# A decoder layer on one Trainium2 core: more of the up-projection's first half done ahead, and the modulation weights asked for by running estimates

## The chip, the cores and the metric

The kernel runs on one core of a Trainium2 chip. The metric is the device time of one execution in microseconds (us). The kernel before takes 1207.88 us (median of 3 runs, 1207.71 to 1208.54).

The engines have short names: PE is the matrix engine, PEld its loading of stationary operands, DVE the vector engine, ACT the scalar engine, SP the engine that issues the transfers. Each engine runs its own instructions strictly in the order in which they stand in its stream, and waits on semaphores for the others.

## The reference, cut to what matters

One layer for 256 tokens of width 2048. A conditioning vector gives six rows of modulation (shift, scale, gate, twice). There are two kinds of attention heads, one output projection, and a gated feed-forward part of width 5504 with a causal convolution of width 3.

```python
mod = silu(c) @ w_ada + b_ada                       # 2048 -> 12288 = 96 columns of 128
sh1, sc1, g1, sh2, sc2, g2 = split(mod, 6)
h = rmsnorm(x) * (1 + sc1) + sh1
q_sb, k_sb, v_sb, q_ds, k_ds, v_ds, q_ix, k_ix, w_ix = split(h @ w_in)
o_sb = stick_breaking_attention(q_sb, k_sb, v_sb)   # 8 heads
o_ds = dsa_attention(...)                           # 8 heads, keys chosen by an indexer, top 64
x  = x + g1 * (concat(rmsnorm(o_sb), rmsnorm(o_ds)) @ w_out)
h2 = rmsnorm(x) * (1 + sc2) + sh2
u  = h2 @ w_up                                      # 2 x 5504 columns: 43 pairs of 128 (gate, value)
uc = causal_conv3(u); a = silu(uc_gate) * uc_value
x  = x + g2 * (a @ w_down)
out = rmsnorm(x)
```

## The kernel before

**Matmuls.** Every large product is taken in fp32r as three matmuls: high by high part, high by low, low by high. A weight load is 1 MB, a tile of 128 x 2048. `split` cuts it in halves of 128 x 1024: ACT casts the high part (L145), DVE subtracts for the low part (L146), each into one of three buffers.

**Transfers.** All weight loads stand in one queue of SP in program order, with four buffers (`load`, L135 to L138). A load is issued when the buffer's former user is done.

**Modulation.** It is 96 columns, in groups of four. A column in DVE's form (`ada`, L216) is one 1 MB load `wa` and one DVE instruction over 128 x 2048 (L218). A group in PE's form (`ada_pe`, L187, for the groups listed in `PEG`) is four 1 MB loads `wg`, each with matmuls of 512 columns into `ap` (L195), then a copy on ACT, four transposes into `aq` (L203) and a small DVE sum. Both forms bring 4 MB per group. Which ones come when is set by `pump`: at its step i it emits as many columns and quarters as the strings of `PLAN` say, and after their end as `RATE` says. `need(j)` emits whatever is still missing.

**Order of the stages.** Projection pass 0 over half of the contraction (wA0 to wA7), with B, V and QK of that half. Then pass 1 (wA8 to wA15), B1, and the indexer with its top-k on DVE (`rel`, L548, L571, L572). V10 and V11 follow, then the sparse attention (`kdsp`, `qdsp`, `lg`), and QK8 to QK15 with the eight stick-breaking heads (`sb_head`, L659). The output projection O begins with the first halves of output tiles m = 0 to 3 from `odh`, `odl`. In the program `rms_b` named `rsb` and `norm_o` come next; they make `osh`, `osl` for the second halves. Then come the residual, `r2`, and the modulated `h2`.

**Up-projection U.** Each pair f has two loads, `wU f 0` for k 0 to 7 and `wU f 1` for k 8 to 15. For the first G0 = 8 pairs the first halves are done ahead, each pair in its own PSUM bank, while the later columns of `h2` are still being made. The second halves then add to the same banks. These pairs use `trn`: three matmuls of 256 columns for each k and half. The other pairs use `fold`: one of 512 columns and one of 256, with two banks, and ACT and DVE add the two parts of a bank (L837, L838). After that come the convolution (L844, L848), SiLU, product, and split into `aT`. W, the down-projection, and the final norm end the kernel.

The scheduler arranges each engine's instructions itself from the program and its dependencies, so a step's place in a stream is not its place in the program.

Of the kernel before, what the change touches and what calls it, by code (L numbers as in the profile page):

```python
# [19 lines left out]
P = 128  # L20
# [22 lines left out]

PEG = [4, 40, 48, 76, 52]

PARTS = [8, 8]

PLAN = ("40300000010011011020201102100000000000000010222000110020002020001010003012011002101000000000100000213",
        "00000000000000000000000000000110010000001200000100001200003100000000000000110100001010001000001000000")

RATE = (0.4, 0.7)


@with_exitstack
def layer(ctx: ExitStack, tc: tile.TileContext, a, out):
# [78 lines left out]

    def load(src, n, name):  # L135
        w = wp.tile([P, 2048], F32, name=name, tag="raw", bufs=4)
        DMA.dma_start(out=w[:, 0:n], in_=src)
        return w  # L138
# [10 lines left out]
    def nat(pt, xh, xl, wh, wl, first, last):  # L149

        T.matmul(pt, lhsT=xh, rhs=wh, start=first, stop=False)  # L151
        T.matmul(pt, lhsT=xh, rhs=wl, start=False, stop=False)
        T.matmul(pt, lhsT=xl, rhs=wh, start=False, stop=last)

    def fold(steps):

        for pt, x, wh, _, first, _ in steps:
            T.matmul(pt, lhsT=wh, rhs=x, start=first, stop=False)  # L160
        for pt, x, _, wl, _, last in steps:
            T.matmul(pt[:, 1, :], lhsT=wl, rhs=x[:, 0, :], start=False, stop=last)  # L162

    def trn(pt, xh, xl, wh, wl, first, last):

        T.matmul(pt, lhsT=wh, rhs=xh, start=first, stop=False)  # L166
        T.matmul(pt, lhsT=wh, rhs=xl, start=False, stop=False)  # L167
        T.matmul(pt, lhsT=wl, rhs=xh, start=False, stop=last)  # L168
# [18 lines left out]
    def ada_pe(j0, q, st={}):  # L187
# [3 lines left out]
        pt = st[j0]  # L191
        w = load(a["wg"][PEG.index(j0), q], 2048, f"wg{j0}{q}")
        for j in range(4):
# [22 lines left out]
    def ada(j):  # L216
        w = load(a["wa"][j], 2048, f"wa{j}")
        i = V.scalar_tensor_tensor(out=w, in0=w, scalar=1.0, in1=scb, op0=ALU.mult, op1=ALU.mult,  # L218
                                   accum_out=mod[:, j:j + 1])
        if after[0] is not None:  # L220
            order(i, after[0])
# [79 lines left out]
    def modulate(dh, dl, x, am, rb, sh, name, variant):  # L301

        h = s2([P, S], F32, name)
        if not variant:
            V.scalar_tensor_tensor(out=h, in0=x, scalar=am, in1=rb, op0=ALU.mult, op1=ALU.mult)
            A.activation(dh, h, AF.Identity, bias=sh)
            V.scalar_tensor_tensor(out=dl, in0=h, scalar=sh, in1=dh.bitcast(F32), op0=ALU.add, op1=ALU.subtract)
            return
# [30 lines left out]
    def put(half, dst, src, scale=1.0):  # L339
        if half == 0:  # L340
            if scale == 1.0:
                A.copy(out=dst, in_=src)
            else:
                A.mul(out=dst, in_=src, mul=scale)
        elif scale == 1.0:
            V.tensor_tensor(out=dst, in0=src, in1=dst, op=ALU.add)
# [3 lines left out]
    pending, pend_pe = [], []  # L350
    credit = [0.0, 0.0]
    emitted = set()
# [15 lines left out]

    step = [0]

    def pump():
        i = step[0]
        step[0] += 1
        for c, l in enumerate((pending, pend_pe)):
            if i < len(PLAN[c]):
                n = int(PLAN[c][i])
            else:
                credit[c] += RATE[c]
                n = int(credit[c])
                credit[c] -= n  # L380
            for _ in range(min(n, len(l))):
                emit(l)

# [155 lines left out]
    for t in range(NT):  # L539
# [4 lines left out]
        for g in range(8 // npb):  # L544
# [6 lines left out]
            for par_ in range(2):  # L551
                rl = s2([P, npb, L], F32, f"rl{t}{g}{par_}")
                A.activation(rl, pts[par_].rearrange("p (n l) -> p n l", n=npb), AF.Relu)  # L553
                for j in range(npb):
# [9 lines left out]
                    else:  # L564
                        V.scalar_tensor_tensor(out=sacc[par_], in0=rl[:, j, :], scalar=wix[:, t, h:h + 1],  # L565
                                               in1=sacc[par_], op0=ALU.mult, op1=ALU.add)
        V.tensor_tensor(out=sacc[0], in0=sacc[0], in1=sacc[1], op=ALU.add)
        cur, nxt = sacc
        for r in range(8):
# [26 lines left out]
    for t in range(NT):  # L596
# [29 lines left out]
        for g in range(2):  # L626
# [6 lines left out]
            for j in range(4):  # L633
                h = 4 * g + j
                A.activation(od[:, h, t * P:(t + 1) * P], pv[:, j, :], AF.Copy, scale=par[:, PDG + h:PDG + h + 1])
        pump()
    for w_ in (4, 2):
# [6 lines left out]
    def norm_o(o, rb_, oh, ol):  # L644
        for h in range(0, NH, 4):
# [3 lines left out]
            A.copy(out=oh[:, sl, :], in_=o[:, sl, :])  # L649
            V.tensor_tensor(out=ol[:, sl, :], in0=o[:, sl, :], in1=oh[:, sl, :].bitcast(F32), op=ALU.subtract)  # L650

    norm_o(od, rdb, odh, odl)
# [5 lines left out]

    def sb_head(h):  # L659
        q = qk[h // 4][:, (h % 4) * 2, :]  # L660
        k = qk[h // 4][:, (h % 4) * 2 + 1, :]
# [65 lines left out]
    def resid(dst, acc, gate, res, sqsum, k, name):  # L727

        resid_i[0] = V.scalar_tensor_tensor(out=dst, in0=acc, scalar=gate, in1=res, op0=ALU.mult, op1=ALU.add)  # L729
        if k == 0:  # L730
# [56 lines left out]
    aT = []  # L787

    G0 = 8
    uacc = {}  # L790

    def do_U(f, i):

        if i == 0:
            uacc[f] = [bank(f"U{f}{gv}") for gv in range(2)] if f >= G0 else bank(f"U{f}")
        w = load(a["wU"][f, i], 2048, f"wU{f}{i}")
        for gv in range(2):
# [6 lines left out]
            for j in range(8):  # L804
# [5 lines left out]
                else:  # L810
                    trn(uacc[f][:, gv, :], x[:, 0, :], x[:, 1, :], wh[:, sl], wl[:, sl], k == 0 and gv == 0,
                        k == KT - 1 and gv == 1)
            fold(steps)
# [7 lines left out]
    for f in range(G0):  # L821
        do_U(f, 0)
        pump()
        if f >= 3:
# [3 lines left out]
    for f in range(FT):  # L828
# [3 lines left out]
        acc = uacc.pop(f)  # L832
        pump()
        if f >= G0:
# [4 lines left out]
        else:  # L839
            u = acc  # L840
        uc = s2([P, 2, S], F32, f"uc{f}")
# [119 lines left out]
```

## Time and profile before

| what | value |
|---|---|
| median of 3 runs | 1207.88 us |
| profiled execution, its own time | 1209.0 us |
| its span from first to last instruction | 1207.2 us |
| mean granted PE clock | 0.982 |
| PE busy | 1154.3 us, 7120 matmuls |
| DVE busy | 886.8 us |
| ACT busy | 630.6 us |
| loads `wa` / `wg` | 76 / 20 of 1 MB each |
| bytes read | 300.24 MB |

A busy time is a sum over the whole span; matmuls are pipelined, so a stretch in which PE is busy throughout can still hold fewer matmuls than it could. The chain of waits names, from the last instruction backward, what each step waited for. In the timeline a row's brackets give the idle time of the engine before the instruction, and the instruction that ended it.

### The profile page before, as it was taken

The numbers are of one execution on the slowest core, as the hardware profiler recorded it, in microseconds if no ns is written. First come the engines' busy times: TensorE is split into PE (matmuls) and PEld (weight loads), VectorE is DVE, ScalarE is ACT, GpSimd is POOL, SyncE is SP. The second block draws the span as 40 slices with busy tenths as digits, with TensorE's granted clock in tenths as the row PEclk, the third lists the DMA queues.
The fourth block names the chain that finished last, engine by engine and source line by source line (L and its number), as shares of the span: only waits on it lengthen the run. The fifth ranks groups of instructions, "written<-read, shape, count | busy, mean of one in ns | idle before, by whom it ended". The sixth has DMA issues, their size and how long they took to land.

```text
span 1207.2 us, 17866 instructions
## 1 busy us (share of the span) xinstructions
PE 1154.3 (96%) x7120; PEld 1015.3 (84%) x7120; DVE 886.8 (73%) x1267; ACT 630.6 (52%) x1004; POOL 0.2 (0%) x4
## 2 busy tenths in 40 slices
PE   3699999899999998999999999999999999999996
PEld 2478997668879998999888888888888888888885
DVE  4876788699868888878799878787787645555553
ACT  3356554448566445466555555555555544444441
POOL 0000000000000000000000000000000000000000
PEclk9799999899999998999999999999999999999998
DMA  8988999758788896865578657566565555545531
GB/s 309 375 328 311 333 333 353 283 192 326 284 298 331 287 358 247 325 247 212 198 276 300 241 207 266 205 232 237 210 227 191 188 197 179 200 180 189 195 140 69
DMA packets 43282, 303.48 MB, mean 251 GB/s; under 512 B 4928, under 2 KB 5440, under 8 KB 7232
## 3 DMA queue, kind: packets, MB, share of 16 engines
q1 hardware_dynamic: 43200, 302.35, 68.3%
q8 instruction: 55, 0.90, 0.3%
q14 instruction: 27, 0.22, 0.0%
HBM read 300.24 MB, written 2.10 MB: 250 GB/s over the span
## 4 chain that ended last, share of the span: by engine, by line
PE 88%; DVE 5%; ACT 3%; DMA 2%; issue 1%; SPq 0%; DVEq 0%; ACTq 0%
PE U L160 21%; PE W L160 13%; PE U L162 11%; PE W L162 7%; PE U L166 3%; PE U L167 3%; PE U L168 3%; PE O L166 3%; PE O L168 3%; PE O L167 3%; PE QK L166 2%; PE QK L167 2%; PE QK L168 2%; DVE wa L218 2%; PE ap L195 1%
## 5 line engine op out<-in xcount | busy, mean ns | idle before, releaser
L218 DVE SCALAR_TENSOR_TENSOR wa<-wa,scb 128x2048 f32<-128x2048 f32 x76 | 173.4, 2284 | 5.3 <-DMA wa<-wa 5.2
L848 DVE SCALAR_TENSOR_TENSOR uc<-u,par,uc 128x255 f32<-128x255 f32 (+1 forms) x140 | 66.4, 480 | 17.6 <-ACT uc L844 15.7
L844 ACT ACTIVATE uc<-u,par 128x256 f32<-128x256 f32 x70 | 42.0, 600 | 40.3 <-DVE u L838 40.3
L838 DVE TENSOR_TENSOR u<-U,u 128x256 f32<-128x256 f32 x70 | 29.2, 417 | 0.7 <-ACT u L837 0.7
L316 ACT ACTIVATE amul<-mod,b,par 128x1 f32<-128x1 f32 x32 | 12.0, 385 | 29.2 <-DVE wa L218 29.2
L837 ACT COPY u<-U 128x256 f32<-128x256 f32 x70 | 25.3, 362 | 0.0
L195 PE MATMUL ap<-wg,csil 128*32 128x512 f32 x160 | 23.4, 640 | 0.6 <-DMA wg<-wg 0.3
L883 DVE SCALAR_TENSOR_TENSOR x1T<-W,mod,x1T 128x256 f32<-128x256 f32 x16 | 7.7, 484 | 21.9 <-PE W L162 21.9
L319 ACT ACTIVATE mod<-mod,par 128x1 f32<-128x1 f32 x32 | 8.7, 294 | 24.0 <-DVE wa L218 23.1
L855 ACT CAST aT<-uc 128x256 fp32r<-128x256 f32 x43 | 17.4, 404 | 3.1 <-DVE uc L854 3.1
L854 DVE TENSOR_TENSOR uc<-uc 128x256 f32<-128x256 f32 x43 | 18.1, 421 | 1.0
L850 ACT ACTIVATE uc<-uc 128x256 f32<-128x256 f32 x43 | 17.8, 415 | 0.4 <-DVE uc L848 0.4
L856 DVE TENSOR_TENSOR aT<-uc,aT 128x256 fp32r<-128x256 f32 x43 | 18.0, 418 | 0.0
L848 DVE SCALAR_TENSOR_TENSOR uc<-U,par,uc 128x255 f32<-128x255 f32 (+1 forms) x32 | 15.2, 478 | 1.1 <-ACT uc L844 0.6
L734 ACT ACTIVATE x2q<-x1T 128x256 f32<-128x256 f32 x15 | 6.2, 416 | 14.6 <-DVE x1T L729 14.4
L195 PEld LDWEIGHTS ap<-wg,csil 128*32 128x32 f32 x160 | 4.3, 114 | 9.2 <-issue 6.9
L548 PE MATMUL rel<-ws,qixT 64*128 64x128 f32 (+1 forms) x64 | 9.9, 392 | 1.5 <-ACT rl L553 1.5
L276 PE MATMUL cb<-ident,csil 128*128 128x128 f32 x16 | 3.6, 423 | 7.6 <-DMA ident<-ident 7.6
L151 PE MATMUL A<-wA00h,hh 128*128 128x512 f32 x4 | 2.5, 669 | 8.5 <-ACT hh L311 8.5
L565 DVE SCALAR_TENSOR_TENSOR scw<-rl,wix,scw 128x128 f32<-128x128 f32 (+1 forms) x28 | 10.4, 408 | 0.0
L679 ACT ACTIVATE sbt<-sbt 128x384 f32<-128x384 f32 x8 | 4.2, 526 | 11.8 <-DVE sbt L678 11.8
L729 DVE SCALAR_TENSOR_TENSOR x1T<-O,mod,xT 128x256 f32<-128x256 f32 x16 | 7.0, 478 | 4.2 <-PE O L168 4.2
(2810 smaller groups left out, 4030.4 us busy)
## 6 DMA issues: line engine op xcount, KB each, us to landing
wU<-wU SPq DMA_DIRECT2D x86, 1024.0 KB, 4.8
wa<-wa SPq DMA_DIRECT2D x76, 1024.0 KB, 6.2
wD<-wD SPq DMA_DIRECT2D x43, 1024.0 KB, 4.6
wg<-wg SPq DMA_DIRECT2D x20, 1024.0 KB, 6.9
wA<-wA SPq DMA_DIRECT2D x16, 1024.0 KB, 7.2
wQK<-wQK SPq DMA_DIRECT2D x16, 1024.0 KB, 7.2
wO<-wO SPq DMA_DIRECT2D x16, 1024.0 KB, 6.5
xT<-xT SPq DMA_DIRECT2D x4, 512.0 KB, 6.0
```

Source lines behind the costliest of these rows:

```text
L160: T.matmul(pt, lhsT=wh, rhs=x, start=first, stop=False)
L162: T.matmul(pt[:, 1, :], lhsT=wl, rhs=x[:, 0, :], start=False, stop=last)
L166: T.matmul(pt, lhsT=wh, rhs=xh, start=first, stop=False)
L167: T.matmul(pt, lhsT=wh, rhs=xl, start=False, stop=False)
L168: T.matmul(pt, lhsT=wl, rhs=xh, start=False, stop=last)
L195: T.matmul(pt[32 * j:32 * j + 32, :], lhsT=csil[:, k:k + 1].to_broadcast([P, 32]), rhs=w[:, j * 512:(j + 1) * 512], start=q == 0, stop=q == 3)
L218: i = V.scalar_tensor_tensor(out=w, in0=w, scalar=1.0, in1=scb, op0=ALU.mult, op1=ALU.mult, accum_out=mod[:, j:j + 1])
L837: A.copy(out=u[:, gv, :], in_=acc[gv][:, 1, :])
L838: V.tensor_tensor(out=u[:, gv, :], in0=acc[gv][:, 0, :], in1=u[:, gv, :], op=ALU.add)
L844: A.activation(uc[:, gv, :], u[:, gv, :], AF.Identity, scale=par[:, PCW + 3 * i + 2:PCW + 3 * i + 3], bias=par[:, PCB + i:PCB + i + 1])
L848: V.scalar_tensor_tensor(out=uc[:, gv, sft:S], in0=u[:, gv, 0:S - sft], scalar=par[:, o:o + 1], in1=uc[:, gv, sft:S], op0=ALU.mult, op1=AL ...
L854: V.tensor_tensor(out=uc[:, 1, :], in0=uc[:, 0, :], in1=uc[:, 1, :], op=ALU.mult)
```

## The change

- `PEG` shrinks from [4, 40, 48, 76, 52] to [4, 40, 44]: twelve quarters on PE in place of twenty, and 84 columns on DVE in place of 76. Group 44 goes to PE, groups 48, 76 and 52 to DVE.
- `PLAN`, `RATE` and the counted steps go. `load` calls `pump` ahead of each weight load. `pump` now emits up to two items, by three running sums of the program: PE's, DVE's and the transfers' estimated time. `spend` adds estimates at the places where work is written. Several separate calls of `pump` go.
- G0 becomes 20. A first half done ahead leaves its bank: ACT copies it to an SBUF tile `ut` (five tiles of four pairs), and after the second half DVE adds the bank to it.

```diff
-PEG = [4, 40, 48, 76, 52]
+PEG = [4, 40, 44]
-PLAN = ("40300000010011011020201102100000000000000010222000110020002020001010003012011002101000000000100000213",
-RATE = (0.4, 0.7)
+G0 = 20
...
-    def load(src, n, name):
+    clk = {"pe": 0.0, "dve": 0.0, "dma": 8.0}
+
+    def spend(pe=0.0, dve=0.0):
+        clk["pe"] += pe
+        clk["dve"] = max(clk["dve"], clk["pe"] - 10.0) + dve
+
+    def load(src, n, name, weight=True):
+        if weight:
+            pump()
+        clk["dma"] = max(clk["dma"], clk["pe"] - 14.0) + 3.04 * n / 2048
+        if weight:
+            clk["pe"] = max(clk["pe"], clk["dma"] + 5.0)
+            spend(0.0, 2.45 * n / 2048)
         w = wp.tile([P, 2048], F32, name=name, tag="raw", bufs=4)
         DMA.dma_start(out=w[:, 0:n], in_=src)
         return w
...
     def trn(pt, xh, xl, wh, wl, first, last):
+        spend(0.36)
         T.matmul(pt, lhsT=wh, rhs=xh, start=first, stop=False)
...
     def ada(j):
-        w = load(a["wa"][j], 2048, f"wa{j}")
+        w = load(a["wa"][j], 2048, f"wa{j}", False)
+        spend(0.0, 2.4)
...
     def pump():
-        i = step[0]
-        step[0] += 1
-        for c, l in enumerate((pending, pend_pe)):
-            if i < len(PLAN[c]):
-                n = int(PLAN[c][i])
-            else:
-                credit[c] += RATE[c]
-                n = int(credit[c])
-                credit[c] -= n
-            for _ in range(min(n, len(l))):
-                emit(l)
+        for _ in range(2):
+            if clk["dma"] + 11.5 > clk["pe"]:
+                return
+            if pending and clk["dve"] + 6.0 <= clk["pe"]:
+                emit(pending)
+            elif pend_pe:
+                emit(pend_pe)
             else:
+                return
...
-    G0 = 8
-    uacc = {}
+    uacc, ut = {}, []
     def do_U(f, i):
-        if i == 0:
-            uacc[f] = [bank(f"U{f}{gv}") for gv in range(2)] if f >= G0 else bank(f"U{f}")
+        if f < G0:
+            uacc[f] = bank(f"U{f}{i}")
+        elif i == 0:
+            uacc[f] = [bank(f"U{f}{gv}") for gv in range(2)]
...
-                    trn(uacc[f][:, gv, :], x[:, 0, :], x[:, 1, :], wh[:, sl], wl[:, sl], k == 0 and gv == 0,
-                        k == KT - 1 and gv == 1)
+                    trn(uacc[f][:, gv, :], x[:, 0, :], x[:, 1, :], wh[:, sl], wl[:, sl], j == 0 and gv == 0,
+                        j == 7 and gv == 1)
...
     for f in range(G0):
         do_U(f, 0)
-        pump()
+        if f % 4 == 0:
+            ut.append(b8([P, 4, 2, S], F32, f"ut{f}"))
+        A.copy(out=ut[-1][:, f % 4, :, :], in_=uacc.pop(f))
...
         acc = uacc.pop(f)
-        pump()
+        spend(0.0, 3.8 if f >= G0 else 3.5)
...
         else:
-            u = acc
+            u = ut[f // 4][:, f % 4, :, :]
+            V.tensor_tensor(out=u, in0=acc, in1=u, op=ALU.add)
```

Below, rows of the instruction streams: the line, the instruction, output and inputs by their tiles' names, the shape, and how many stand in a row. Line numbers of the changed kernel are its own.

PE, at the indexer, before: among the matmuls of `rel` (the indexer's scores) stand those of V1000, the first half-load of V10.

```order
L548 MATMUL rel_1966<-ws,qixT 128x256
L548 MATMUL rel_1967<-ws,qixT 128x256
L548 MATMUL rel_1980<-ws,qixT 128x256 x2
L151 MATMUL V_2295<-V1000h,hh_1352 128x512
L548 MATMUL rel_1981<-ws,qixT 128x256 x2
L548 MATMUL rel_1994<-ws,qixT 128x256 x2
L152 MATMUL V_2295<-V1000l,hh_1352 128x512
L153 MATMUL V_2295<-V1000h,hl_1353 128x512
L151 MATMUL V_2296<-V1000h,hh_1352 128x512
```

The same place in the changed kernel: after the last `rel` come modulation quarters, and then `kdsp`, `qdsp`, `aq` and `lg`, which are the sparse attention after the top-k.

```order
L562 MATMUL rel_2014<-ws,qixT 128x256
L562 MATMUL rel_2015<-ws,qixT 128x256
L209 MATMUL ap_1965<-wg_2055,csil 32x512 x4
L209 MATMUL ap_1965<-wg_2061,csil 32x512 x4
L209 MATMUL ap_1965<-wg_2188,csil 32x512 x4
L599 MATMUL kdsp<-ident,ws 128x128
L606 MATMUL qdsp_2096<-ident,qds 128x128 x4
L606 MATMUL qdsp_2102<-ident,qds 128x128 x4
L599 MATMUL kdsp<-ident,ws 128x128
L217 MATMUL aq_2196<-ident,rw_2194 128x128 x4
L162 MATMUL V_2327<-V1000h,hh_1361 128x512
L163 MATMUL V_2327<-V1000l,hh_1361 128x512
```

All of V10 but these two matmuls has moved behind `lg`.

PE, in O, before: `rsbp` (the sums for the norm of the stick-breaking heads) stands between the first halves of output tiles 0 and 1, and `rsbb` (its spread over partitions) inside tile 2, in two pieces of the stream:

```order
L168 MATMUL O_3204<-odh,wO001l 128x256
L195 MATMUL ap_3184<-wg_3266,csil 32x512 x4
L115 MATMUL rsbp<-nones,ws 128x1 x2
L203 MATMUL aq_3274<-ident,rw_3272 128x128 x4
L166 MATMUL O_3205<-odh,wO100h 128x256
```

```order
L168 MATMUL O_3205<-odh,wO101l 128x256
L166 MATMUL O_3206<-odh,wO200h 128x256
L167 MATMUL O_3206<-odl,wO200h 128x256
L129 MATMUL rsbb<-ident,rsby 128x128 x2
L168 MATMUL O_3206<-odh,wO200l 128x256
```

In the changed kernel both stand behind the last first half, with nothing between them and nothing ahead of the second halves, which read `osh` and `osl`.

```order
L180 MATMUL O_3140<-odl,wO301h 128x256
L181 MATMUL O_3140<-odh,wO301l 128x256
L112 MATMUL rsbp<-nones,ws 128x1 x2
L126 MATMUL rsbb<-ident,rsby 128x128 x2
L179 MATMUL O_3137<-osh,wO010h 128x256
L179 MATMUL O_3138<-osh,wO110h 128x256
L180 MATMUL O_3137<-osl,wO010h 128x256
```

DVE at that place in the changed kernel: between `rsbv` (the first step after `rsbp`) and the rest of the chain stands a modulation column.

```order
L156 TENSOR_TENSOR wO110l<-wO_3476,wO110h 128x1024
L118 TENSOR_SCALAR rsbv<-rsbp 128x2
L233 SCALAR_TENSOR_TENSOR wa_3603,mod<-wa_3603,scb 128x2048
L121 SCALAR_TENSOR_TENSOR rsbl<-rsby 128x2
L122 TENSOR_TENSOR rsbl<-rsbl,rsbv 128x2
L123 SCALAR_TENSOR_TENSOR rsby<-rsbl,rsby 128x2
L663 TENSOR_TENSOR os<-os,rsb 128x1024 x2
L666 TENSOR_TENSOR osl<-os,osh 128x1024 x2
```

DVE at the entry of U, before: `g_0` (the first column of `h2`) follows the last step of `r2` directly.

```order
L146 TENSOR_TENSOR wU100l<-wU_4414,wU100h 128x1024
L121 TENSOR_SCALAR r2v<-r2p 128x2
L124 SCALAR_TENSOR_TENSOR r2l<-r2y 128x2
L125 TENSOR_TENSOR r2l<-r2l,r2v 128x2
L126 SCALAR_TENSOR_TENSOR r2y<-r2l,r2y 128x2
L305 SCALAR_TENSOR_TENSOR g_0_4304<-x1T_3485,amul,r2b 128x256
```

In the changed kernel a modulation column has come between, and `wU100l` stands inside the chain.

```order
L118 TENSOR_SCALAR r2v<-r2p 128x2
L156 TENSOR_TENSOR wU100l<-wU_4347,wU100h 128x1024
L121 SCALAR_TENSOR_TENSOR r2l<-r2y 128x2
L122 TENSOR_TENSOR r2l<-r2l,r2v 128x2
L123 SCALAR_TENSOR_TENSOR r2y<-r2l,r2y 128x2
L233 SCALAR_TENSOR_TENSOR wa_4269,mod<-wa_4269,scb 128x2048
L321 SCALAR_TENSOR_TENSOR g_0_4229<-x1T_3410,amul,r2b 128x256
```

The column was not there before; `wU100l` stood ahead of `r2v`.

## Rows read from the trace of the kernel before

**Rows 1.** The page: span, busy time, and the chain that ended last, by engine.

```profile
span 1207.2 us, 17866 instructions
PE 1154.3 (96%) x7120; PEld 1015.3 (84%) x7120; DVE 886.8 (73%) x1267; ACT 630.6 (52%) x1004; POOL 0.2 (0%) x4
PE 88%; DVE 5%; ACT 3%; DMA 2%; issue 1%; SPq 0%; DVEq 0%; ACTq 0%
```

**Rows 2.** Stretches: length, busy time (and count) by engine, granted PE clock, DMA share, GB/s.

```profile
30.00:60.00 30.00, 19.03 (x62) 14.39 (x63) 25.88 (x27) 11.66 (x21) 0.00 (x0) 0.72 0.95 375
460.00:470.00 10.00, 5.50 (x36) 5.04 (x35) 7.40 (x18) 4.74 (x12) 0.00 (x0) 0.82 0.72 286
510.00:520.00 10.00, 10.00 (x85) 10.00 (x84) 6.71 (x8) 4.51 (x6) 0.00 (x0) 1.00 0.98 389
540.00:570.00 30.00, 30.00 (x230) 29.00 (x229) 27.27 (x44) 19.05 (x33) 0.00 (x0) 1.00 0.64 233
```

**Rows 3.** Timeline of PE at pass 0 of A: start, duration, instruction, [idle before, releaser].

```profile
34.75 1.22 PE L151 MATMUL A<-wA00h,hh 128*128 128x512 f32 x2 [8.55 <-ACT hh L311]
49.04 1.22 PE L151 MATMUL A<-wA10h,hh 128*128 128x512 f32 x2 [6.18 <-ACT wA10h L145]
```

**Rows 4.** Timelines at the indexer: PE, then DVE.

```profile
244.85 0.40 PE L151 MATMUL V<-V1002h,hh 128*128 128x512 f32 x1
...
247.37 0.39 PE L153 MATMUL V<-V1002h,hl 128*128 128x512 f32 x1
```

```profile
231.09 1.22 DVE L146 TENSOR_TENSOR V1000l<-V10w,V1000h 128x1024 fp32r<-128x1024 f32 x1 [3.48 <-ACT V1000h L145]
```

**Rows 5.** Modulation on PE: timeline of PE, waits of SP's queue, a piece of the chain.

```profile
222.09 1.92 PE L195 MATMUL ap<-wg,csil 128*32 128x512 f32 x16
341.06 0.60 PE L203 MATMUL aq<-ident,rw 128*128 128x128 f32 x4
```

```profile
SPq L137 <- PE ap L195: 59.3, 20, 14.9
```

```profile
313.81 6.50 DMA wQK<-wQK
```

**Rows 6.** Chain of `rsb`: timelines of PE, DVE and ACT; the page's group of DVE's modulation columns.

```profile
373.19 0.61 PE L115 MATMUL rsbp<-nones,ws 128*128 128x1 f32 x4
...
380.45 0.38 PE L129 MATMUL rsbb<-ident,rsby 128*128 128x128 f32 x2
```

```profile
381.27 1.22 DVE L647 TENSOR_TENSOR os<-os,rsb 128x1024 f32<-128x1024 f32 x1 [0.41 <-ACT rsb L132]
```

```profile
380.86 0.37 ACT L132 COPY rsb<-rsbb 128x256 f32<-128x256 f32 x1 [1.45 <-PE rsbb L129]
382.53 1.05 ACT L649 CAST osh<-os 128x1024 fp32r<-128x1024 f32 x1 [0.34 <-DVE os L647]
```

```profile
L218 DVE SCALAR_TENSOR_TENSOR wa<-wa,scb 128x2048 f32<-128x2048 f32 x76 | 173.4, 2284 | 5.3 <-DMA wa<-wa 5.2
```

**Rows 7.** Entry of U: timelines of DVE and PE.

```profile
466.28 1.26 DVE L305 SCALAR_TENSOR_TENSOR g<-x1T,amul,r2b 128x256 f32<-128x256 f32 x3 [0.93 <-ACT r L132]
```

```profile
467.69 0.55 PE L166 MATMUL U<-h,wU000h 128*128 128x256 f32 x1 [1.85 <-ACT h L306]
...
468.69 0.41 PE L166 MATMUL U<-h,wU000h 128*128 128x256 f32 x1
...
473.33 0.28 PE L166 MATMUL U<-h,wU000h 128*128 128x256 f32 x1
```

**Rows 8.** Half-blocks of U: timeline of PE, `trn`; pieces of the chain, `fold`.

```profile
484.60 0.28 PE L166 MATMUL U<-h,wU201h 128*128 128x256 f32 x1
...
487.48 0.28 PE L166 MATMUL U<-h,wU300h 128*128 128x256 f32 x1
```

```profile
562.52 1.84 PE U L160 x8
565.32 1.84 PE U L160 x8
```

More of the change, by code (lines that the diff above doesn't have):

```diff
@@ L40 @@
 PW = 520
-PEG = [4, 40, 48, 76, 52]
+PEG = [4, 40, 44]
 PARTS = [8, 8]
-PLAN = ("40300000010011011020201102100000000000000010222000110020002020001010003012011002101000000000100000213",
-        "00000000000000000000000000000110010000001200000100001200003100000000000000110100001010001000001000000")
-RATE = (0.4, 0.7)
+G0 = 20
 @with_exitstack
@@ L149, in nat @@
     def nat(pt, xh, xl, wh, wl, first, last):
+        spend(3 * (pt.shape[-1] + 32) / 2400)
         T.matmul(pt, lhsT=xh, rhs=wh, start=first, stop=False)
@@ L155, in fold @@
     def fold(steps):
+        spend(0.35 * len(steps))
         for pt, x, wh, _, first, _ in steps:
@@ L191, in ada_pe @@
         pt = st[j0]
-        w = load(a["wg"][PEG.index(j0), q], 2048, f"wg{j0}{q}")
+        w = load(a["wg"][PEG.index(j0), q], 2048, f"wg{j0}{q}", False)
+        spend(0.85 if q < 3 else 1.4)
         for j in range(4):
@@ L303, in modulate @@
         h = s2([P, S], F32, name)
+        spend(0.0, 0.9)
         if not variant:
@@ L344, in put @@
                 A.mul(out=dst, in_=src, mul=scale)
-        elif scale == 1.0:
+            return
+        spend(0.0, 0.53)
+        if scale == 1.0:
             V.tensor_tensor(out=dst, in0=src, in1=dst, op=ALU.add)
@@ L350, in layer @@
     pending, pend_pe = [], []
-    credit = [0.0, 0.0]
     emitted = set()
@@ L367, in emit @@
             emitted.update(range(j, j + 4))
-    step = [0]
     def pump():
-        i = step[0]
-        step[0] += 1
-        for c, l in enumerate((pending, pend_pe)):
-            if i < len(PLAN[c]):
-                n = int(PLAN[c][i])
-            else:
-                credit[c] += RATE[c]
-                n = int(credit[c])
-                credit[c] -= n
-            for _ in range(min(n, len(l))):
-                emit(l)
+        for _ in range(2):
[5 more added lines that the diff above has]
+                emit(pend_pe)
+            else:
+                return
     def need(j):
@@ L567, in layer @@
         V.tensor_tensor(out=sacc[0], in0=sacc[0], in1=sacc[1], op=ALU.add)
+        spend(8.0, 20.0)
         cur, nxt = sacc
@@ L635, in layer @@
                 A.activation(od[:, h, t * P:(t + 1) * P], pv[:, j, :], AF.Copy, scale=par[:, PDG + h:PDG + h + 1])
+        spend(10.0, 8.0)
         pump()
@@ L650, in norm_o @@
             V.tensor_tensor(out=ol[:, sl, :], in0=o[:, sl, :], in1=oh[:, sl, :].bitcast(F32), op=ALU.subtract)
+            spend(0.0, 2.5)
     norm_o(od, rdb, odh, odl)
@@ L659, in sb_head @@
     def sb_head(h):
+        spend(3.0, 1.6)
         q = qk[h // 4][:, (h % 4) * 2, :]
@@ L727, in resid @@
     def resid(dst, acc, gate, res, sqsum, k, name):
+        spend(0.0, 0.9)
         resid_i[0] = V.scalar_tensor_tensor(out=dst, in0=acc, scalar=gate, in1=res, op0=ALU.mult, op1=ALU.add)
```

## The prediction

> **What bounds the kernel now.** I read the page first. PE is busy for 1154.3 of 1207.2 us, and the chain of waits is PE for 88% [rows 1]. So the time is PE's own work plus the few places where PE waits, and a change of DVE's or the queue's load counts only where PE then stands still. Next I read stretches, to see which limit each has [rows 2]: at 30 to 60 us PE is busy 19.03 of 30.00 while the transfers run at a share of 0.95; at 460 to 470 us PE works 5.50 of 10.00; in 510 to 520 and 540 to 570 us PE is full. Third I read PE's timeline around the idle places, for what ended each. There are three: pass 0 of A, which waits for weights [rows 3]; the indexer, where DVE picks the keys [rows 4]; and the entry of U, where PE waits for `h2` [rows 7]. A fourth could be there and is not: the norm chain `rsb`, whose start and end on PE are 7.3 us apart with O's matmuls between [rows 6]. Last I set beside these places what the streams of the changed kernel hold there.
>
> The profiled execution took 1209.0 us, 1.1 above the median of 1207.88. The sum is made against 1209.0, and 1.1 is taken off at the end.
>
> **Part 1: pass 0 of A, -2.** wA1 now stands behind four columns and no longer behind six. One load at 375 GB/s [rows 2] is 1.049 MB / 375 = 2.8 us, so it comes some 5.6 us sooner and most of the 6.18 us wait before wA10 goes [rows 3]. But up to wA7 the queue carries the same 24 loads in both kernels, so the end of the pass is still set by the transfers. I take -2: more of PE's work is then done when the last weights land. The bounds are -6.2 (the whole wait) and +2.8, since three more columns then stand ahead of wA8, of which PE's full queue of work hides all but one.
>
> **Part 2: the indexer, +6.** Before, V10's four half-blocks filled PE's waits for the top-k. Twelve of their matmuls run from 244.85 to 247.37, 0.229 us apart [rows 4], so 48 are 11.0 us. In the new stream all but two of them stand behind `lg`, which needs the top-k's result. In their place stand seven modulation quarters, where three stood before. Sixteen matmuls, two quarters, take 1.92 us [rows 5], so the four extra fill 3.8. On the other side DVE no longer waits 3.48 us for V1000's cast [rows 4]; I count 1.9 of that as an earlier start. 11.0 - 3.8 - 1.9 = 5.3, and some 0.7 for a PE clock that falls in waits, as it did to 0.82 at 460 to 470 us [rows 2]. The bounds are +3 (the displaced V10 fills later waits of the softmax) and +11 (it fills none, and the queue, which now holds seven `wg` ahead of V10's load, adds to it).
>
> **Part 3: QK and the heads, -11.** Groups 48, 76 and 52 leave PE and 44 comes, so eight quarters go: 8 x 0.96 = 7.7 us. Two sets of four transposes go, 0.60 each and overlapped with the next matmul [rows 5]; I count 1.0 for both. DVE, which takes the eight columns, is busy 27.27 of 30 us at 540 to 570 us [rows 2], but the program moves its columns to U's first half and to later pairs, where four subtractions of a pair are spread over two pieces. So much for work. For waits: the queue stood 59.3 us, in 20 waits, behind `ap` [rows 5], and one late load in this stage, 6.50 us, is a piece of the chain [rows 5]. Eight quarters less are 8 MB less here. I take 2.3 of the 6.50. Sum -11; bounds -7.7 (no wait goes) and -15.2 (the 6.50 goes whole).
>
> **Part 4: `rsb` in O, +11.** Before, `rsbp` ran at 373.19 and `rsbb` at 380.45 and PE never stopped [rows 6]. Now both stand behind the last first half, and the next matmul needs `osh`, soon `osl`. What lies between is bare. I add DVE's way from the last matmul of O301, whose buffers wO110 waits for: cast and subtraction of wO110, 1.05 + 1.22; `rsbv`, 0.15; one modulation column, 2.28 [rows 6]; three small steps, 0.6; `rsbb`, 0.4, and its copy 0.37 up to 381.27 - 380.86 = 0.4 [rows 6]; `os` twice at 1.14; the first half of `osl`, 1.14. Together 9.6 us. The cast of `osh` lies beside the second `os`. PE has about 1.1 us of work in it (`rsbp`, `rsbb`, the matmuls that need `osh` alone), so 8.5 are lost. After such a wait PE is slow: behind the 1.85 us wait at 467.69 the matmuls from 468.69 to 473.33 come 0.211 us apart, 22 of them [rows 7], against 2.88/24 = 0.120 [rows 8]. 26 such matmuls from the restart cost 26 x 0.091 = 2.4. So +11. What is queued behind the waiting matmuls on PE is all of the second halves; nobody else can go ahead of them. The bounds are +6 (the column and wO110 come early enough: 9.6 - 2.28 - 1.05 - 1.22 - 1.1 = 4.0, and 2.4 of slow clock) and +13 (a column's load that is not there, 2.8).
>
> **Part 5: entry of U, +4.4.** Before, `g_0` began 0.93 us after DVE's last work and PE restarted at 467.69 [rows 7]. Now a column of 2.28 us stands ahead of `g_0`, and ACT casts wU100 inside the chain, about 1.0. That is 3.3 at the start. PE then eats U0 and U1 at the pace at which DVE makes `h2`, and two more columns stand among `g_6`, `h_6`, `g_7`, `h_7` where one stood (another 2.28), of which half is hidden by PE's slow clock in this stretch. Bounds +2 (only the first column, partly hidden) and +6.9 (three columns in full).
>
> **Part 6: `trn` in place of `fold` for 12 pairs, +4.2.** 12 pairs have 48 half-blocks. One in `trn` takes 487.48 - 484.60 = 2.88 us; one in `fold` 565.32 - 562.52 = 2.79 [rows 8]. 48 x 0.087 = 4.2 us, on PE, in a stretch where PE is full, so nothing hides it. The copies to `ut` go to ACT, busy 19.05 of 30 at 540 to 570 us [rows 2]; DVE's two adds of 256 columns become one of 512. What hides them is PE's 5.76 us per pair. In the first halves a pair asks for a column and a weight load, 2.1 MB in 5.76 us = 364 GB/s; 510 to 520 us carried 389 at a share of 0.98 [rows 2], so it is covered, with little to spare. Bounds: +3 and +5 for PE alone; cover failing is a rival.
>
> The Trainium skill, in TensorE: Matmul & The Clock Gate, section Step-by-step: what each phase is for, says that throughput is "purely `N cycles`", one column each. `trn` and `fold` both move 768 columns for each k and half, so by this rule part 6 would be 0 and the time 4.2 lower. The rows show 2.88 against 2.79 for the same columns; the trace does not agree, and the rows are used.
>
> **Sum.** -2 + 6 - 11 + 11 + 4.4 + 4.2 = +12.6; 1209.0 + 12.6 - 1.1 = 1220.5.
>
> **Rivals.** *Faster.* The transfers' relief is worth more: part 1 at -6, part 3 at -13 (both waits and work), and the new waits are short because the columns in them run early: part 2 at +3, part 4 at +6, part 5 at +2. With part 6 that is -3.8: 1207.88 - 3.8 = 1204. For it speaks that PE waited in this kernel mostly for weights, and 8 MB leave a stage where the queue stood behind `ap` [rows 5]; against it, that the columns stand in the streams ahead of the chain's own steps, and DVE cannot pass them. It is decided at `rsb`: a wait of under 4 us there.
>
> *About the same.* The chain of `rsb` costs 6 and the indexer 3, since V10's work fills PE's waits after `lg`, and the rest is as forecast: -2 + 3 - 11 + 6 + 2 + 4.2 = +2.2, 1210. For it: work that is moved behind a wait is not lost if a later wait takes it up. Against: `rsb` has nothing behind it that could.
>
> *Much slower.* U's first halves become bound by the transfers, or second halves by DVE. At the 286 GB/s of 460 to 470 us [rows 2] a pair would take 2.1 MB / 286 = 7.3 us, 1.6 over PE's; six of the 20 pairs at that pace are 10 us. 1220.5 + 10 = 1230. For it: DVE at 27.27 of 30 and the transfers at a share of 0.98 [rows 2]. Against: the columns are gone from the second halves, and PE was full at 389 GB/s.
>
> *It does not do what it says:* the estimates could drift and leave columns to the `need` ahead of a stage, in a burst. Before U there stand three columns in a row, where two stood; that is part 5, and no larger burst is in the streams.
>
> **Chances and range.** My forecast 0.60, much slower 0.16, about the same 0.12, faster 0.12. What a measurement can tell from no change is 0.2%, 2.4 us: 1205.5 to 1210.3. Faster 0.13, within 0.12, slower 0.75. The range takes in the forecast with its bounds (the uncertain parts spread by some 9 us together) and reaches toward both ends, 1207 to 1230. The forecast's own range is 1213 to 1228.
>
> **What would show it.** In the new profile: an idle time of PE of 6 to 9 us ahead of the first matmuls of O with `osh`, released by the cast or subtraction of `os`; a later start of U0 relative to the end of O, by 3 us; `lg` later than V10 would let it, with PE idle under the top-k; half-blocks of 2.88 us for 20 pairs, with PE full; and fewer waits of PE under QK8 to QK15. I am wrong if PE passes from O301 to O010 within 3 us, or if PE has holes in U's first halves. If U's stretch is full and O has its hole, but the sum is off by more than 5, it is parts 1 to 3 that were mis-sized.

## The result, and the profile after

The changed kernel takes 1236.33 us (median of 4 runs, 1233.29 to 1239.22) against 1208.21 for the kernel before (1207.71 to 1209.79). The ratio is 1.023, with an interval of 1.021 to 1.0251. The forecast was 1220.5, with a range of 1207 to 1230: the side was right, the size was 12 of 28 us, and the time lies above the range.

The page after, the lines that answer to [rows 1] and to the last of [rows 6]:

```profile
span 1231.4 us, 18529 instructions
...
PE 1151.4 (94%) x7432; PEld 1033.7 (84%) x7432; DVE 902.8 (73%) x1277; ACT 632.0 (51%) x998; POOL 0.2 (0%) x4
...
PE 66%; DVE 15%; DMA 10%; issue 6%; ACT 3%; SPq 0%; DVEq 0%; ACTq 0%
...
L233 DVE SCALAR_TENSOR_TENSOR wa<-wa,scb 128x2048 f32<-128x2048 f32 x84 | 192.1, 2287 | 34.0 <-DMA wa<-wa 33.8
```

PE is busy 2.9 us less than before, and the span is 24.2 us longer: the change did take work off PE, and PE waits more than it saves. The chain of waits has fallen from 88% PE to 66%, and DVE's columns now wait 33.8 us for their loads, in place of 5.2. Since DVE works in order, what stands behind a late column on DVE is late too.

The stages in the two profiled executions, each up to the start of the PE matmul named (us). Pass 0 counts from the start of the span; of wU42 and wD42 the start of the last row of eight matmuls is taken.

| stage, and where it ends | before | after | more | forecast |
|---|---|---|---|---|
| pass 0, last of wA7 | 92.6 | 94.8 | +2.2 | -2 (part 1) |
| B, V, QK of pass 0, pass 1, last of wA15 | 120.3 | 120.8 | +0.5 | 0 |
| indexer, attention, heads, O, first r2p | 248.1 | 257.5 | +9.4 | +6 (parts 2, 3, 4) |
| entry of U, last of wU7 first half | 55.1 | 59.8 | +4.7 | +4.4 (part 5) |
| rest of U, last of wU42 | 436.3 | 443.9 | +7.6 | +4.2 (part 6) |
| W, last of wD42 | 240.2 | 240.2 | 0.0 | 0 |

The stretches with the new holes, then a full one and one of the late pairs (columns as in [rows 2]):

```profile
240.00:260.00 20.00, 8.28 (x51) 4.26 (x48) 20.00 (x80) 8.06 (x13) 0.00 (x0) 0.78 0.50 196
380.00:400.00 20.00, 13.23 (x108) 12.78 (x107) 12.99 (x16) 6.92 (x11) 0.00 (x0) 0.87 0.77 293
400.00:420.00 20.00, 18.70 (x141) 18.40 (x142) 13.65 (x16) 8.78 (x12) 0.00 (x0) 0.88 0.43 155
480.00:500.00 20.00, 15.57 (x109) 15.11 (x110) 17.28 (x28) 10.01 (x19) 0.00 (x0) 0.83 0.62 220
580.00:600.00 20.00, 20.00 (x169) 20.00 (x169) 15.69 (x17) 11.01 (x16) 0.00 (x0) 1.00 0.91 331
860.00:880.00 20.00, 18.86 (x109) 16.51 (x109) 16.65 (x25) 12.50 (x20) 0.00 (x0) 1.00 0.80 283
```

At 240 to 260 us DVE is full and PE mostly idle: that is the top-k without V10. At 380 to 420 us neither is full: a chain that goes back and forth. At 580 to 600 us, in the first halves done ahead, PE is full while the transfers carry 331 GB/s.

PE's timeline at the holes, which answers to [rows 4], [rows 6] and [rows 7]:

```profile
254.41 0.45 PE L599 MATMUL kdsp<-ident,ws 128*128 128x128 f32 x1 [8.16 <-DVE ws L314]
...
257.33 0.45 PE L606 MATMUL qdsp<-ident,qds 128*128 128x128 f32 x1 [2.48 <-DVE qds L314]
...
392.07 0.50 PE L112 MATMUL rsbp<-nones,ws 128*128 128x1 f32 x4
...
397.38 0.44 PE L126 MATMUL rsbb<-ident,rsby 128*128 128x128 f32 x1 [4.81 <-DVE rsby L123]
...
400.84 0.58 PE L179 MATMUL O<-osh,wO010h 128*128 128x256 f32 x1 [2.80 <-ACT osh L665]
...
402.10 0.58 PE L180 MATMUL O<-osl,wO010h 128*128 128x256 f32 x1 [0.47 <-DVE osl L666]
...
482.66 0.55 PE L179 MATMUL U<-h,wU000h 128*128 128x256 f32 x1 [2.73 <-ACT h L322]
...
492.14 0.39 PE L180 MATMUL U<-h,wU000h 128*128 128x256 f32 x1 [1.50 <-DVE h L323]
...
861.35 0.39 PE L174 MATMUL U<-h,wU3210l 128*128 128x256 f32 x1 [1.14 <-DVE wU3210l L156]
```

Each bracket is a wait that the kernel before did not have, or had smaller. DVE's timeline under the second one shows why `rsbb` came late:

```profile
393.27 1.22 DVE L156 TENSOR_TENSOR wO110l<-wO,wO110h 128x1024 fp32r<-128x1024 f32 x1 [1.64 <-ACT wO110h L155]
394.42 0.15 DVE L118 TENSOR_SCALAR rsbv<-rsbp 128x2 f32<-128x2 f32 x1
394.48 2.28 DVE L233 SCALAR_TENSOR_TENSOR wa<-wa,scb 128x2048 f32<-128x2048 f32 x1
396.69 0.08 DVE L233 DVE_READ_ACCUMULATOR wa<-wa,scb 128x1 f32 x1
396.69 0.16 DVE L121 SCALAR_TENSOR_TENSOR rsbl<-rsby 128x2 f32<-128x2 f32 x1
```

wO110's subtraction and a modulation column stand ahead of 0.16 us of work for which PE waits.

### The profile page after: what moved, and what is told of

The parts are those of the page before. It is cut to its first block, busy times and chain, and to the rows that moved or that the text cites. A ratio compares the mean times of both kernels' runs of the same rounds, so it can differ in the third digit from the quotient of the medians.

```text
span 1231.4 us, 18529 instructions
## 1 busy us (share of the span) xinstructions
PE 1151.4 (94%) x7432; PEld 1033.7 (84%) x7432; DVE 902.8 (73%) x1277; ACT 632.0 (51%) x998; POOL 0.2 (0%) x4
## 4 chain that ended last, share of the span: by engine, by line
PE 66%; DVE 15%; DMA 10%; issue 6%; ACT 3%; SPq 0%; DVEq 0%; ACTq 0%
PE W L172 13%; DMA wa<-wa 8%; PE W L174 7%; PE U L180 6%; PE U L181 6%; PE U L179 6%; PE U L172 5%; DVE wa L233 4%; PE U L174 3%; PE QK L181 2%; PE QK L180 2%; PE QK L179 2%; DVE uc L871 2%; PE O L180 1%; PE O L181 1%
## 5 line engine op out<-in xcount | busy, mean ns | idle before, releaser
L233 DVE SCALAR_TENSOR_TENSOR wa<-wa,scb 128x2048 f32<-128x2048 f32 x84 | 192.1, 2287 | 34.0 <-DMA wa<-wa 33.8
L867 ACT ACTIVATE uc<-u,par 128x256 f32<-128x256 f32 x46 | 27.6, 601 | 42.6 <-DVE u L860 42.5
L871 DVE SCALAR_TENSOR_TENSOR uc<-u,par,uc 128x255 f32<-128x255 f32 x92 | 42.8, 478 | 7.7 <-ACT uc L867 7.0
L335 ACT ACTIVATE mod<-mod,par 128x1 f32<-128x1 f32 x32 | 9.1, 293 | 49.1 <-DVE wa L233 48.1
L871 DVE SCALAR_TENSOR_TENSOR uc<-ut,par,uc 128x255 f32<-128x255 f32 (+1 forms) x80 | 33.2, 477 | 0.0
L867 ACT ACTIVATE uc<-ut,par 128x256 f32<-128x256 f32 x40 | 21.8, 593 | 0.0
L860 DVE TENSOR_TENSOR u<-U,u 128x256 f32<-128x256 f32 x46 | 19.2, 417 | 0.0
L863 DVE TENSOR_TENSOR ut<-U,ut 128x512 f32<-128x512 f32 x20 | 13.8, 691 | 6.4 <-PE U L181 6.4
L845 ACT COPY ut<-U 128x512 f32<-128x512 f32 x20 | 11.7, 583 | 11.9 <-PE U L181 11.8
L859 ACT COPY u<-U 128x256 f32<-128x256 f32 x46 | 16.6, 360 | 0.0
L209 PE MATMUL ap<-wg,csil 128*32 128x512 f32 x96 | 14.4, 672 | 1.8 <-DMA wg<-wg 1.5
L697 ACT ACTIVATE sbt<-sbt 128x384 f32<-128x384 f32 x8 | 4.2, 526 | 13.4 <-DVE sbt L696 13.4
```

The costliest lines, as they stand in the source:

```text
L860: V.tensor_tensor(out=u[:, gv, :], in0=acc[gv][:, 0, :], in1=u[:, gv, :], op=ALU.add)
L867: A.activation(uc[:, gv, :], u[:, gv, :], AF.Identity, scale=par[:, PCW + 3 * i + 2:PCW + 3 * i + 3], bias=par[:, PCB + i:PCB + i + 1])
L871: V.scalar_tensor_tensor(out=uc[:, gv, sft:S], in0=u[:, gv, 0:S - sft], scalar=par[:, o:o + 1], in1=uc[:, gv, sft:S], op0=ALU.mult, op1=AL ...
```

## The experiments

Two theories stood against each other. **Moved work**: each new hole has its own cause in the order of one engine's stream, and goes when that order is mended. **The queue**: the new requests come late or in rows, so that mending a place only moves the wait. For each run the ratio to the kernel before, run beside it, is given with its interval; "stage" is the one from the end of pass 1 to `r2p`, 248.1 us before.

**The changed kernel again.**

> The changed kernel once more, beside the three below. Theory (moved work): its time is the kernel before plus 24 to 31 us, with the same holes of PE: under the top-k, between the first and second halves of O, and at the entry of U. Rival (the queue): the holes come from transfers that land late, so their places and sizes differ from run to run by several us.

1233.19 us, ratio 1.0218 (1.0195 to 1.0241). The stage is 257.4, against 257.5, and the first hole is the same to the hundredth:

```profile
254.31 0.45 PE L599 MATMUL kdsp<-ident,ws 128*128 128x128 f32 x1 [8.16 <-DVE ws L314]
```

So the holes belong to the streams. Two things differed: the entry of U took 61.1 us and not 59.8, and the rest of U 440.5 and not 443.9, with no hole in the late pairs.

**`rsb` early.**

```diff
     for m in range(4):
         do_O(acc[m], m, 0, odh, odl)
+        if m == 0:
+            (rsb: rms_b and norm_o, moved up from below)
         pump()
-    (the same lines of rsb, behind the loop)
```

> The changed kernel with rsb's sums, its norm and the norm of os written behind the first of the four first halves of O and no longer behind the fourth. Theory (moved work): the 8.8 us between rsbp and the first matmul with osh, and the slow clock behind them, go: 9 to 11 us faster than the changed kernel, and nothing else moves. Rival (the queue): the second halves' loads are late as well, so less than 4 us are won and the hole shows again, then released by a cast of wO.

1225.56 us, 1.0155 (1.014 to 1.017); the stage falls by 8.3, to 249.1. PE's timeline has no wait left at the three places:

```profile
384.57 0.28 PE L112 MATMUL rsbp<-nones,ws 128*128 128x1 f32 x2
...
386.81 0.27 PE L126 MATMUL rsbb<-ident,rsby 128*128 128x128 f32 x1
...
395.41 0.28 PE L179 MATMUL O<-osh,wO010h 128*128 128x256 f32 x1
```

The gain is a little under what was expected, and no hole came up behind it: moved work.

**V10 first, without filling.**

```diff
+    hold[0] = True       # behind pass 1: pump() emits nothing
...
     for g in range(2):
         do_V(last_p, g)
+    hold[0] = False
```

> The changed kernel with no modulation asked for between the end of pass 1 and the loads of V11: V10's loads then stand behind three wg and not behind seven, as in the kernel before. Theory (moved work): V10's matmuls come back into PE's wait for the top-k: PE's lost time between 220 and 280 us falls from 22.6 to some 13, and the kernel is 6 to 10 us faster than the changed one; the four quarters of group 44 then cost nothing new in the QK stage. Rival (the queue): the quarters moved to QK make its loads late and the gain is under 3 us.

1229.39 us, 1.0174 (1.0154 to 1.0195). The stage falls by 5.3 and the time by 3.8, where 6 to 10 were expected: V10 is back in the hole, but most of group 44's quarters now stand behind it, two of them among the heads, where PE is full. The entry of U is also longer, 63.2. Both theories had a part of it.

**V10 first, the quarters between V10 and V11.**

```diff
-    for g in range(2):
-        do_V(last_p, g)
+    do_V(last_p, 0)
+    while pend_pe:
+        emit(pend_pe)
+    do_V(last_p, 1)
+    hold[0] = False
```

> The changed kernel with V10's loads ahead of group 44's four quarters, and those quarters between V10 and V11, in the hole, and nothing else. Theory (moved work): the stage from the end of pass 1 to r2, 257.4 us in the changed kernel, falls by the 10 that separate rsb early (249.1) from the kernel mended but for h2 (239.0), to 247 to 249: 1222 to 1226 us. Rival (the two mends only work together, since the hole at rsb takes what is won at the indexer): the stage stays above 253 and the time above 1229.

1220.83 us, 1.0091 (1.0068 to 1.0113). The stage is 247.5: 9.9 us less, where 10 were expected; the time is a little under the 1222 to 1226. The wait under the top-k has gone from 8.16 to 0.68, while the wait for `osh` at `rsb` stays as it was. The two add up: 8.3 and 9.9 make 18.2, and with both mended (below) the stage is 18.4 shorter.

```profile
257.76 0.30 PE L601 MATMUL kdsp<-ident,ws 128*128 128x128 f32 x1 [0.68 <-DVE ws L314]
...
392.10 0.58 PE L179 MATMUL O<-osh,wO010h 128*128 128x256 f32 x1 [2.80 <-ACT osh L667]
```

**The three groups alone, on the kernel before.**

```diff
-PEG = [4, 40, 48, 76, 52]
+PEG = [4, 40, 44]
```

> The kernel before with the three groups [4, 40, 44] on PE, and nothing else changed: the plan's strings stay, and columns that they do not reach are asked for in a row of eleven behind wU10. Theory (moved work): the stage of the heads loses 8 to 10 us of PE's work; rsb's steps, which in this stream too stand behind the last first half of O, give back 6 to 9; the row of eleven columns, 31 us of transfers, then costs 5 to 15 in U. Sum: 5 us faster to 15 slower than the kernel before. Rival (the queue): the heads win nothing and the time is over 15 us slower.

1229.4 us, 1.0188 (1.017 to 1.0206): the rival's figure, but the heads did win. The stage falls to 243.8 although `rsb` now stands bare here too, with waits of 6.6 us, so that hole comes from the groups alone, not from the estimates. The rest of U is 23.5 us longer, nearly all of it one wait, for the eleven columns asked for in a row:

```profile
379.03 0.24 PE L115 MATMUL rsbp<-nones,ws 128*128 128x1 f32 x1 [2.05 <-DVE ws L689]
...
384.33 0.58 PE L166 MATMUL O<-osh,wO010h 128*128 128x256 f32 x1 [2.80 <-ACT osh L649]
...
533.46 0.58 PE L166 MATMUL U<-h,wU010h 128*128 128x256 f32 x1 [20.90 <-ACT wU010h L145]
```

**20 pairs ahead alone, on the kernel before.** (Its diff is that of the change for `do_U`, `ut` and G0.)

> The kernel before with the first halves of 20 pairs done ahead and their sums kept in SBUF, and nothing else changed; its plan and its five groups on PE stay. Theory (moved work): up to the entry of U nothing changes; 12 pairs in trn cost 4.2 us, and U has no holes of PE beyond that: 1211 to 1213 us. Rival (the second halves are bound by DVE or the first by the transfers): PE has holes in U's first 115 us and the time is over 1216.

1224.46 us, 1.0131 (1.011 to 1.0151). That is the rival's figure, and the rest of U is 16.8 longer. But it does not tell the two apart as it was meant to, since the holes are not where the rival has them, in U's first 115 us: the plan's counts now fall at other loads, and columns in rows of two and three stand in the second halves, where PE waits 2.56 and 1.77 for weights:

```profile
613.69 0.58 PE L166 MATMUL U<-h,wU510h 128*128 128x256 f32 x1 [2.56 <-ACT wU510h L145]
...
616.25 0.58 PE L168 MATMUL U<-h,wU410l 128*128 128x256 f32 x1 [1.77 <-DVE wU410l L146]
```

**`h2` free of columns.** (On the kernel with `rsb` early.)

```diff
     for m in range(8):
+        while pending and pending[0][0] % 16 < min(8, m + 3):
+            emit(pending)
...
     queue((80, 84, 88, 92))
-    pump()
...
     for k in range(8):
         h2_make(k)
+    after[0] = h_last[0]     # columns asked for from here on come behind h_7
```

> The kernel with rsb early, and with the 16 columns that the first half of h2 needs asked for evenly during O, so that DVE has no modulation column between r2 and h_7. Theory (moved work): from r2's first matmul to the end of U's first half of pair 7 it takes 55 to 56 us as in the kernel before, in place of 60; 4 to 5 us faster than with rsb early alone. Rival (the queue): the columns moved into O make O's loads late; what is won at the entry of U shows as PE's waits in O, and the time stays within 2 us.

1233.47 us, 1.0203 (1.0187 to 1.022). The entry of U takes 55.4 in place of 60.4, as expected, and PE's wait there is back at 1.85. But O has new holes, and the stage is 16.1 longer than with `rsb` early: the rival was right on the place. Neither was right on the sum: the time is 7.9 us above that of `rsb` early (5.8 by the two ratios), where the one theory had 4 to 5 less and the other the same within 2.

```profile
429.51 0.38 PE L179 MATMUL O<-odh,wO400h 128*128 128x256 f32 x1 [2.02 <-ACT wO400h L155]
...
487.22 0.55 PE L179 MATMUL U<-h,wU000h 128*128 128x256 f32 x1 [1.85 <-ACT h L324]
```

**Everything mended.** To V10's gap and to `h2` free of columns come the old order of the columns in pass 0 (not shown) and, in place of `rsb` early, work for PE between `rsb`'s steps:

```diff
+    def ahead(m):
+        acc.append(ps(f"O{m}", tag="att"))
+        do_O(acc[m], m, 0, odh, odl)
+        pump()
-    rms_b([sqs], NH * HD, rsb, "rsb", "att")
+    rms_b([sqs], NH * HD, rsb, "rsb", "att", lambda: ahead(4))   # runs it ahead of rsbb
...
     norm_o(os_, rsb, osh, osl)
-    pump()
+    ahead(5)
...
-        if m >= 4:
+        if m >= 6:
```

> The changed kernel with every new wait mended: pass 0's columns in the order of before, V10's loads ahead of group 44's quarters and those still ahead of V11's, h2's columns during O, and the first halves of output tiles 4 and 5 put between rsb's steps as PE's work. Theory (moved work): relative to the changed kernel -2, -9, -5, -10: 1206 to 1212 us, the kernel before or a little slower. Rival (the queue): the waits come back in other places, above 1218.

1219.32 us, 1.0092 (1.0075 to 1.0109): the rival's figure. The columns in rows again make holes in O, of 1.08 to 2.02 us. Without that mend:

> The changed kernel with every new wait mended but the one at the entry of U: h2's columns are left where the estimates put them. Theory (moved work): O loses its holes of some 7 us between 412 and 433 us, since no columns come in rows there; the entry gives back 5: 1213 to 1218 us, against 1219.3. Rival (DVE is full in O anyway): the holes stay, above 1220.

1209.47 us, 1.0006 (0.9993 to 1.0019), better than expected. The stage is 239.0, 9.1 below the kernel before, and the wait at `rsb` is 0.75. The entry of U takes 56.2 without that mend.

**The groups mended on the kernel before**, with 20 pairs ahead, one column asked for per first half, and `rsb` filled by the first halves of tiles 4 and 5:

> The kernel before, its plan kept up to U, with the three groups on PE, 20 pairs ahead with one column asked for per pair, and the first halves of output tiles 4 and 5 put between rsb's steps. Theory (moved work): pass 1 to the end of O gains what PEG alone gained there, 4, and the 9 of its hole at rsb; U costs 4 more: 1197 to 1203 us, faster than both. Rival (DVE sets the heads): the eight columns more on DVE lengthen the heads' chain, and PE waits for it in O: 1205 to 1212.

1212.12 us, 1.0028 (1.0017 to 1.0039), at the edge of the rival's range, but not by its mechanism: in the profiled execution, the fastest of the ten, the stage is 234.7, 13.4 below the kernel before, which is the 4 and the 9 expected. What was missed is U, 13.1 longer, with PE waiting where the plan's leftover counts ask for columns in the second halves. So these were taken out, and 16 columns asked for in 20 first halves:

```diff
-        if pending:
+        if pending and f % 5 < 4:
             emit(pending)
...
-        pump()
+        if f >= G0:
+            step[0] = len(PLAN[0])
+            pump()
-RATE = (0.4, 0.7)
+RATE = (0.75, 0.7)
```

> As PEG mended, but no modulation is asked for in the second halves of the pairs done ahead: 16 columns spread over the 20 first halves, the last 16 over the 23 fold pairs. Theory (moved work): the stage of U, 449.4 us in PEG mended against 436.3 before, falls to 440.5, the 4.2 us of trn alone; all else as in PEG mended: 1198 to 1203 us, faster than the kernel before. Rival (second halves bound by DVE whatever stands there): U stays above 446 and the time above 1206.

1203.09 us, 0.9959 (0.9946 to 0.9971): faster than both kernels, just above the range that was expected. The rest of U takes 440.5 us, the 4.2 of `trn` and nothing else. The page and the wait at `rsb`:

```profile
PE 90%; DVE 5%; ACT 2%; DMA 2%; issue 1%; SPq 0%; DVEq 0%; ACTq 0%
```

```profile
392.60 0.38 PE L169 MATMUL O<-osl,wO010h 128*128 128x256 f32 x1 [0.75 <-DVE osl L652]
```

**The same with 16 pairs ahead** (G0 = 16, a column for each pair, RATE 0.62).

> The same with 16 pairs ahead, one column for each. Theory (moved work): 8 pairs more than before in trn and not 12, 2.8 us in place of 4.2: 1 to 2 us faster than with 20. Rival (the queue): a column and a weight for each pair without a gap is more than the transfers carry beside h2's work on DVE; PE has holes in U's first halves and it is slower than with 20.

1203.89 us, 0.9965 (0.9953 to 0.9977), not to be told from 20 pairs. PE has small waits of 0.4 us in the first halves, released by DVE, and U takes 441.5: the four pairs saved are eaten up. This profiled execution is the slowest of the six, 3.3 us above their median, so its waits need not be in the others.

The running estimates alone, with the five groups on PE and 8 pairs ahead, were not run.

## Why the prediction was wrong, step by step

The waits at the indexer, at `rsb` and at the entry of U were named at the right places, and each of them showed. What failed is the size, in four places that all went one way (pass 0, the credits at the indexer, the gain in the heads, the cover of U's late pairs), and the range. Taken all at their upper bounds the six parts give +31.0, or 1239; the range ended at 1230, as if some of them would cancel.

**Part 2, the indexer (+6): mis-sized, 9.9.** The gross loss was right, 11.0 us of V10 pushed out of the hole. The step that failed is what was set against it, 3.8 for four extra quarters that fill the hole and 1.9 for DVE's earlier start. There were no four extra quarters. From the end of pass 1 to the first `lg` seven quarters ran on PE in the kernel before and eight in the changed one, and behind the last `rel` there are three in both. The row of the changed kernel (24 matmuls, eight a quarter):

```profile
243.46 2.78 PE L209 MATMUL ap<-wg,csil 128*32 128x512 f32 x24
```

So about 1 us could be credited. And the hole's end is DVE's, not PE's. DVE is busy for the whole of 240 to 260 us in both kernels; this is the stretch before:

```profile
240.00:260.00 20.00, 17.98 (x93) 11.48 (x91) 20.00 (x83) 8.32 (x13) 0.00 (x0) 0.97 0.43 160
```

From the end of pass 1 to the first `lg` it takes 48.6 us after and 49.1 before, so the start gave 0.5. With V10 back in the hole and the quarters of group 44 behind it the stage is 9.9 us shorter.

**Part 3, QK and the heads (-11): near.** With both holes mended the stage is 9.1 us shorter in the changed kernel's order, and 12.1 to 13.4 in the order of the kernel before. What makes the 3 to 4 us between the two orders is open. It lies ahead of the heads: from the end of pass 1 to the first QK matmul of this stage it takes 75.6 us in the kernel mended but for `h2` and 69.3 in the spread one with 20 pairs, and 3.3 less behind that. The heads' own chain is not what makes it: from the first to the last sum of squares it takes 51.6 us in the changed kernel (326.66 to 378.30) and 46.5 before (325.51 to 372.01), but 51.4 in the spread one too, which has five modulation columns on DVE in it, where the changed one has eight and the kernel before four.

**Part 4, `rsb` (+11): right in kind, 8.3.** From `rsbp` to the first matmul with `osl` 10.0 us passed (392.07 to 402.10), where 9.6 had been worked out; in the order shown, with wO110's subtraction and the column inside. PE's waits in it are 4.81, 2.80 and 0.47, 8.1 together, where 8.5 were forecast. The term that was mis-sized is the slow clock behind them: it was to last for 26 matmuls, 2.4 us, and lasted for 12 (402.10 to 404.82), 1.3 us more than at 0.120 each. Mending it won 8.3. Parts 2 to 4 then add up to 9.9 - 9.1 + 8.3 = 9.1, and 9.4 was measured.

**Part 5, the entry (+4.4): right,** 4.7, with the column ahead of `g_0` as forecast:

```profile
479.04 2.29 DVE L233 SCALAR_TENSOR_TENSOR wa<-wa,scb 128x2048 f32<-128x2048 f32 x1
```

With DVE free of columns there, the stage is as before (55.4 to 55.1). That the figure came so close has some luck in it: the second run of the same kernel has 6.0, and in the two kernels with V10 first, whose edits are far from this place, it is 8.1 and 1.9.

**Part 6, `trn` (+4.2): the price right, the cover wrong.** Where U has no holes it is 440.5 us against 436.3, three times (the second run of the changed kernel, `h2` free, spread over 20): 4.2. (As printed, [rows 8] gives 2.80 for a `fold` half-block and so 3.8; the forecast's 2.79 fits better.) By the rule of the Trainium skill that was weighed (TensorE: Matmul & The Clock Gate, Step-by-step: what each phase is for) it would have been 0; these three runs do not agree with it. But the profiled execution lost 3.4 more, and the one with V10 in its gap 4.8, in the fold pairs, which the prediction had left as they were. There a column now stands at every second load, and when its transfer is late DVE waits for it with the weights' subtraction behind it. PE's wait of 1.14 us at 861.35, shown above, has this on DVE ahead of it:

```profile
857.13 2.29 DVE L233 SCALAR_TENSOR_TENSOR wa<-wa,scb 128x2048 f32<-128x2048 f32 x1 [2.95 <-DMA wa<-wa]
...
860.08 1.22 DVE L156 TENSOR_TENSOR wU3210l<-wU,wU3210h 128x1024 fp32r<-128x1024 f32 x1
```

The rival "much slower" had this mechanism, but in the first and second halves done ahead, which are full.

**Part 1, pass 0 (-2): the sign was wrong,** +2.2, and 0.5 more in pass 1. The step that failed is that the end of the pass is set by the transfers alone, and that an earlier wA1 leaves less work behind them. wA1 did come sooner, and its wait fell from 6.18 to 1.34 us. But the columns that it passed were needed for the next steps: PE now waits for `hh` ahead of wA20 and wA30, where it had not.

```profile
44.17 1.20 PE L162 MATMUL A<-wA10h,hh 128*128 128x512 f32 x4 [1.34 <-ACT hh L327]
...
53.55 1.22 PE L162 MATMUL A<-wA20h,hh 128*128 128x512 f32 x2 [3.60 <-ACT hh L327]
...
62.93 1.59 PE L162 MATMUL A<-wA30h,hh 128*128 128x512 f32 x4 [2.14 <-ACT hh L327]
```

From the first matmul with wA00 to the last of wA7 the kernel before takes 57.8 us, and 60.0 is what all six profiled executions with the new order take. With the old order of the columns the kernel mended in all places takes 58.4 and the one mended but for `h2` 57.9, and PE's waits for `hh` at these two places are gone. So some 2 us hang on the order.

**From one execution to the median.** 1.1 was taken off, since the profiled execution of the kernel before lay above its median. That of the changed kernel lay 3.0 below its own: its four runs spread over 6 us, and U's late pairs differ from run to run (no loss beyond `trn` to 3.4 us in two executions of the same kernel). That is 4.1 us of the miss, the luck of which execution was profiled, and no row of before could show it.

Of the sum, the miss of 15.8 us is thus: part 1 with pass 1 4.7, part 2 3.9, part 3 1.9, part 4 -2.7, part 5 0.3, part 6 3.4, the median 4.1; the rest is below one.

## What to carry to other kernels

When work leaves a hole that another engine ends, price its new place in full, and give credit for what is said to come into the hole in its stead only after counting what stood there before. When a scheduler orders an engine that works in sequence, look what becomes of the short chains that the removed work used to hide: keep a block of independent work to stand between their steps, as the first halves of two further tiles did here. Where requests stand in the queue counts: one at a time beside U's weights they cost PE nothing that shows, and in O five more of them, in rows of two to four, cost 16 us. Whether the rows or the number did that was not separated.

## What the runs showed of the hardware

In these streams two matmuls of 256 columns take longer than one of 512: 0.120 us each in `trn`, where the row of eight of 512 in `fold` takes 1.84, or 0.230 each [rows 8].

The clock granted to PE in the changed kernel was 1.00 (2.4 GHz) at 240 to 251 us and 0.50 (1.2 GHz) at 252 to 260, so it fell within the wait of 8.16 us that ends at 254.41; before, with V10 in that hole, it was 0.97 over 240 to 260. At `rsb` it was 0.50 at 396 to 404, where PE waited 4.81, 2.80 and 0.47 us, and 1.00 at 405.5 to 420, where PE is busy throughout.
